# Summing the modulation vectors of a two-layer encoder over partitions: a GpSimd all-reduce in place of TensorE transposes and matmuls with ones

## The chip, the cores and the metric

The kernel runs on one core of a Trainium2 chip. The metric is the device time of one execution in microseconds (us), the median of the runs shown. The engines are named as the profile names them: PE is TensorE, PEld its weight loads, DVE is VectorE, ACT is ScalarE, POOL is GpSimd, and SP is SyncE, whose queue issues all DMAs here.

## What is computed

A bidirectional encoder of two layers on 256 tokens of 1024 channels, in float32. Each layer first makes six modulation vectors of 1024 channels from one conditioning vector `c`, and uses them around a mixer (three kinds of attention) and a SwiGLU feed-forward part:

```python
mod = jax.nn.silu(c) @ ada_w + ada_b                     # (1024,) @ (1024, 6*1024)
sh_m, sc_m, g_m, sh_f, sc_f, g_f = split(mod, 6)         # m = 0 .. 5 in the kernel
h = rms_norm(x, norm_mix_g) * (1 + sc_m) + sh_m
proj = h @ w_in                                          # three attentions and three gates follow
x = x + g_m * (merged @ w_out)
h = rms_norm(x, norm_ffn_g) * (1 + sc_f) + sh_f
gate, up = split(h @ ffn_w_gate_up)
x = x + g_f * ((silu(gate) * up) @ ffn_w_down)
```

## The kernel before, in words

**The stream of weights.** All projections are one list of *items*, each two 128-row chunks of a weight matrix by 512 columns. An item is loaded by SP into one of five `raw` buffers (512 KB), split by ACT into a rounded part `whi` and by DVE into the rest `wlo` (`split_to`, L215 and L216), and read by PE in three matmuls a chunk (L305 to L307) for each of the two token tiles. There are seven buffers of `whi` and of `wlo`, so DVE may split some items ahead of PE. PE works on the second token tile four items behind the first (`LAG = 4`). Two items' worth of steps, one for each token tile, move the counter `cur`; `later(k, fn)` defers a piece of code by `k` such steps. Beside the items stand pieces of attention, put at items by `at`. A scheduler then orders each engine's instructions; every engine works through its own list in order.

**The modulation vectors.** One matrix of 1024 by 1024 belongs to each vector m. It is taken in two halves of 512 columns, and each half in four units (`ada_units`): a unit loads 256 rows into a `raw` buffer of the same five, and DVE multiplies each row chunk by its value of silu(c) and adds it to `acc`, 128 partitions by 512 columns (L137, L139). What is left after the fourth unit is to add the 128 partitions of `acc` (`fin`). Two ways are used:
- m = 0, 1, 3, 4 are needed with the channel on the partition. `col_mod` transposes the four 128-column blocks of `acc` on PE (L121), and DVE adds along the free axis out of PSUM (L123) and adds the bias. This happens `DG = 4` steps later.
- m = 2 and 5 are needed as rows, the same on every partition. `acc` is split into two parts (ACT L215, DVE L216), and PE multiplies both with a matrix of ones (L201, L202), which sums and copies to all partitions at once; DVE adds the bias row out of PSUM (L203).

**Where the units stand.** In each layer the six halves of m = 2, 4, 3 are spread over the items of the gates and attention. Layer 0 then takes the two halves of its m = 5 and the four of layer 1's m = 1 and 0 during its feed-forward part; layer 1 takes the two of its own m = 5 there. That makes 20 halves: 8 as rows, 12 as columns. The first vectors of layer 0 are made by other functions in quarters, at the kernel's start, and are not touched here except for one buffer.

I call the stretches **A** (layer 0's attention, about 90 to 205 us, six halves), **B** (layer 0's feed-forward, about 265 to 375 us, six halves), **C** (layer 1's attention, about 495 to 610 us, a repeat of A with six halves) and **D** (layer 1's feed-forward, about 690 to 780 us, two halves).

**POOL** has little to do: it makes the small reciprocal roots of the norms by a power (L107), the rotary tables, the attention bias, and, right behind A and C, the sums of the three branches (`post_br`, L708), whose result PE transposes (L717).

Of the kernel before, what the change touches and what calls it, by code (L numbers as in the profile page):

```python
# [15 lines left out]
P = 128  # L16
# [16 lines left out]
DO = 2  # L33
DG = 4
DN = 4
# [3 lines left out]
def encoder_kernel(ctx: ExitStack, tc: tile.TileContext, x, consts, cols, rows, ada_b, rpb, ada_w, w_in,  # L39
                   w_uq, w_ukv, w_na, w_mla, w_gqa, w_out, w_gu, w_dn, fng, out):  # L40
    nc = tc.nc

# [1 line left out]
    cpool = ctx.enter_context(tc.tile_pool(name="cpool", bufs=1))  # L44
# [4 lines left out]
    s2p = ctx.enter_context(tc.tile_pool(name="s2p", bufs=2))  # L49
    tmp = ctx.enter_context(tc.tile_pool(name="tmp", bufs=6))  # L50
    ppl = ctx.enter_context(tc.tile_pool(name="ppl", bufs=4))
# [8 lines left out]
    def nm(s):  # L60
        uid[0] += 1
        return f"{s}_{uid[0]}"
# [12 lines left out]

# [1 line left out]
    x_sb = cpool.tile([P, NT, D], F32, name="x_sb")  # L77
# [23 lines left out]
    def colp(l, kind, j0, n):  # L101
        base = KC + l * 64 + {"b": 0, "gm": 48, "gf": 56}[kind]
        return cols_sb[:, base + j0: base + j0 + n]
# [5 lines left out]

# [1 line left out]
    mods = {}  # L111

    def col_mod(l, m, j0, n, acc):
        """Sums acc [128, n*128] over its partitions into columns j0..j0+n of the modulation (channel on partition)."""
        if (l, m) not in mods:
            mods[(l, m)] = modp.tile([P, KC], F32, tag=f"c{m}", name=nm("cm"))
        dst = mods[(l, m)][:, j0:j0 + n]
        ps = tpb()
        pv = ps.rearrange("p (j q) -> p j q", j=4)
        for j in range(n):  # L120
            nc.tensor.transpose(pv[:, j, :], acc[:, j * P:(j + 1) * P], ident)  # L121
        red = sm(4)[:, 0:n]
        nc.vector.tensor_reduce(out=red, in_=pv[:, 0:n, :], op=ALU.add, axis=AX.X)  # L123
        bcol = colp(l, "b", m * KC + j0, n)
        if m in (1, 4):
            r2 = sm(4)[:, 0:n]
            nc.vector.tensor_tensor(out=r2, in0=red, in1=bcol, op=ALU.add)
            g = colp(l, "gm" if m == 1 else "gf", j0, n)
            nc.vector.scalar_tensor_tensor(out=dst, in0=r2, scalar=1.0, in1=g, op0=ALU.add, op1=ALU.mult)
        else:  # L130
            nc.vector.tensor_tensor(out=dst, in0=red, in1=bcol, op=ALU.add)

    def ada_acc(acc, raw, kc0, nk):
# [22 lines left out]
    def ada_quarter_pe(l, m, q, raws):  # L156
# [3 lines left out]
        for kc in range(KC):  # L160
            nc.tensor.matmul(ps[0:1, 0:256], sc[:, kc:kc + 1], raws[(m, kc // 4)][:, kc % 4, :], start=(kc == 0),
                             stop=(kc == KC - 1))
        row = smp.tile([1, 256], F32, tag="row", name=nm("row"), bufs=1)
        nc.scalar.copy(row, ps[0:1, 0:256])
# [6 lines left out]
    def ada_units(l, m, hf, row):  # L171
# [14 lines left out]
        def fin():  # L186
            acc = st["acc"]
            if not row:
                later(DG, lambda: col_mod(l, m, hf * 4, 4, acc))
                return  # L190
            if hf == 0:
                mods[(l, m)] = modp.tile([P, D], F32, tag="G", name=nm("G"), bufs=1)
            bb = t2([P, 512])
            c0 = m * D + hf * 512
            nc.sync.dma_start(bb, ada_b[l, c0:c0 + 512].partition_broadcast(P))
            ah, al = t2([P, 512], F32R), t2([P, 512], F32R)
            split_to(ah, al, acc)

            def b_():
                ps = tpb()  # L200
                nc.tensor.matmul(ps, onesr, ah, start=True, stop=False)  # L201
                nc.tensor.matmul(ps, onesr, al, start=False, stop=True)  # L202
                nc.vector.tensor_tensor(out=mods[(l, m)][:, hf * 512:(hf + 1) * 512], in0=ps, in1=bb, op=ALU.add)  # L203

            later(DG, b_)

        return [unit(u) for u in range(4)]

# [1 line left out]
    def act_tiles():  # L210
# [49 lines left out]

# [1 line left out]
    items = []  # L262
# [22 lines left out]
    def group(units_src, nkc, n, lhs, post, kc0=0, pres=None):  # L285
        """units_src(u): DRAM sources of unit u (two contraction chunks); lhs(t, part, kc): stationary operand."""
        ps = {}
# [37 lines left out]
    def later(k, fn):  # L325
        deferred.append((cur[0] + k, fn))
# [10 lines left out]

    # ================= layers =================
    ssn = {}
# [6 lines left out]
    def layer(l):  # L346
# [4 lines left out]

# [1 line left out]
        def params():  # L353
# [40 lines left out]

# [1 line left out]
        def post_g1(t, ps):  # L396
# [50 lines left out]
        def rope64(dst, tmpv, xin, C, Sg, H):  # L447
            """dst = x*C + swap16(x)*S over H heads of 64"""
            xv = xin.rearrange("p (h d) -> p h d", h=H)
# [125 lines left out]

# [1 line left out]
        def attn_head(branch, h):  # L577
# [115 lines left out]

# [1 line left out]
        st["m"] = {}  # L695
# [37 lines left out]

# [1 line left out]
        def post_res(key, m, after, half=None):  # L735
# [28 lines left out]

# [1 line left out]
        st["hid"] = {}  # L766
# [70 lines left out]

# [1 line left out]
        def spread(units, a, b):  # L839
# [16 lines left out]

# [1 line left out]
    state[0] = {"hT": None}  # L858
# [143 lines left out]
```

## Time and profile before

| what | value |
|---|---|
| time, median of 3 runs | 851.92 us (850.71 to 852.44) |
| span of the profiled execution | 852.1 us |
| PE busy | 809.9 us, 95% |
| DVE busy | 612.1 us, 72% |
| ACT busy | 426.4 us, 50% |
| POOL busy | 85.0 us, 10% |
| DMA, mean rate | 220 GB/s |

The profiled execution has no time of its own besides its span. An engine's busy time is the sum of its instructions' own durations where they don't overlap; an idle engine costs only where something waits for it.

### The profile page before, as it was taken

Reading aid. Unit: us, or ns where it says so; the run is one execution under the profiler, and the core shown is the slowest. Engines: PE = TensorE matmul, PEld = TensorE weight load, DVE = VectorE, ACT = ScalarE, POOL = GpSimd, SP = SyncE. Lnnn points to the kernel's source line nnn. Section 1 sums busy time; section 2 is a strip of 40 time slices with the busy share of each in tenths; the row PEclk is TensorE's granted clock in tenths of the full one; section 3 lists DMA queues with packets and bytes.
Section 4 is the critical chain, followed back from the end, with each engine's and each line's share of the span. In section 5 each row is a group of like instructions: output and inputs, shape, how many; then the busy total and the mean of one; then the engine's idle time right before and its main releaser. Section 6 shows DMA issues by size and latency. Waiting matters only on the chain.

```text
span 852.1 us, 10916 instructions
## 1 busy us (share of the span) xinstructions
PE 809.9 (95%) x3842; PEld 654.0 (77%) x3842; DVE 612.1 (72%) x910; ACT 426.4 (50%) x725; POOL 85.0 (10%) x110
## 2 busy tenths in 40 slices
PE   3779999999999999999999999999999999999996
PEld 2348787888778887788878888788877788888884
DVE  4848998688867878785566698868886666665562
ACT  3346654444366443444457665544437644444341
POOL 1142120002400000000032001000240000000010
PEclk9999999999999999999999999999999999999998
DMA  9968677678555998985774667767755567775531
GB/s 317 348 154 271 188 237 245 221 224 266 178 173 166 317 305 281 308 270 188 207 216 141 178 187 240 248 217 222 259 186 173 178 222 255 249 232 178 191 102 50
DMA packets 112871, 187.21 MB, mean 220 GB/s; under 512 B 14384, under 2 KB 33456, under 8 KB 112816
## 3 DMA queue, kind: packets, MB, share of 16 engines
q1 hardware_dynamic: 112816, 186.51, 69.3%
q8 instruction: 30, 0.49, 0.2%
q14 instruction: 25, 0.20, 0.1%
HBM read 185.44 MB, written 1.05 MB: 219 GB/s over the span
## 4 chain that ended last, share of the span: by engine, by line
PE 76%; DVE 9%; DMA 7%; issue 4%; ACT 3%; POOL 2%; POOLq 0%; DVEq 0%; SPq 0%; ACTq 0%
PE mm L305 21%; PE mm L307 20%; PE mm L306 20%; DMA raw<-in_ada_w_dram 6%; PE tp L598 4%; DVE wlo L216 3%; PE o L654 3%; DVE acc L139 3%; PE tp L633 2%; PE mm L298 1%; ACT tm L246 1%; PE tp L237 1%; PE tp L779 1%; PE tp L121 1%; ACT hi L215 1%
## 5 line engine op out<-in xcount | busy, mean ns | idle before, releaser
L215 ACT CAST whi<-raw 128x1024 fp32r<-128x1024 f32 (+2 forms) x240 | 249.8, 1044 | 266.4 <-PE mm L307 191.4
L216 DVE TENSOR_TENSOR wlo<-raw,whi 128x1024 fp32r<-128x1024 f32 (+2 forms) x240 | 300.0, 1256 | 102.0 <-ACT whi L215 101.6
L305 PE MATMUL mm<-whi,hi 128*128 128x512 f32 (+1 forms) x768 | 306.5, 399 | 0.6 <-ACT hi L215 0.6
L306 PE MATMUL mm<-wlo,hi 128*128 128x512 f32 (+1 forms) x768 | 299.8, 390 | 2.2 <-DVE wlo L216 2.1
L307 PE MATMUL mm<-whi,lo 128*128 128x512 f32 (+1 forms) x768 | 300.1, 391 | 0.7 <-DVE lo L721 0.5
L307 PEld LDWEIGHTS mm<-whi,lo 128*128 128x128 f32 x768 | 144.2, 188 | 32.9 <-DVE lo L216 1.7
L306 PEld LDWEIGHTS mm<-wlo,hi 128*128 128x128 f32 x768 | 144.5, 188 | 30.6 <-DVE wlo L216 3.7
L305 PEld LDWEIGHTS mm<-whi,hi 128*128 128x128 f32 x768 | 144.3, 188 | 30.6 <-issue 2.6
L139 DVE SCALAR_TENSOR_TENSOR acc<-raw,sc,acc 128x512 f32<-128x512 f32 x140 | 104.6, 747 | 37.2 <-DMA raw<-in_ada_w_dram 35.4
L305 PE MATMUL mm<-whi,s 128*128 128x512 f32 (+1 forms) x188 | 73.6, 391 | 0.0
L306 PE MATMUL mm<-wlo,s 128*128 128x512 f32 (+1 forms) x188 | 72.8, 387 | 0.0
L307 PE MATMUL mm<-whi,s 128*128 128x512 f32 (+1 forms) x188 | 72.8, 388 | 0.0
L708 POOL TENSOR_TENSOR tm<-tm,tm 128x512 f32<-128x512 f32 x16 | 28.7, 1793 | 211.1 <-DVE tm L707 205.0
L307 PEld LDWEIGHTS mm<-whi,s 128*128 128x128 f32 x188 | 35.3, 188 | 7.1
L306 PEld LDWEIGHTS mm<-wlo,s 128*128 128x128 f32 x188 | 35.3, 188 | 6.9
L305 PEld LDWEIGHTS mm<-whi,s 128*128 128x128 f32 x188 | 35.3, 188 | 6.8
L384 POOL TENSOR_TENSOR s<-s,con 128x256 f32<-128x256 f32 x16 | 15.6, 1003 | 176.2 <-DMA s<-in_rpb_dram 168.6
L624 ACT ACTIVATE P<-tp,sm,rq 128x256 f32<-128x256 f32 x32 | 17.7, 558 | 27.1 <-DVE sm L619 23.7
L298 PE MATMUL mm<-raw,hF 128*128 128x416 f32 (+1 forms) x64 | 28.6, 599 | 0.0
L237 PE MATMUL tp<-con,tm 128*128 128x128 f32 x64 | 10.1, 313 | 16.7 <-DVE tm L230 16.7
L654 PEld LDWEIGHTS o<-s,PT 128*128 128x128 f32 x192 | 24.2, 191 | 1.1
L107 POOL TENSOR_TENSOR sm<-sm,nhalf 128x1 f32<-128x1 f32 (+2 forms) x22 | 18.3, 833 | 64.4 <-DVE sm L469 33.1
(145 smaller groups left out, 719.4 us busy)
## 6 DMA issues: line engine op xcount, KB each, us to landing
raw<-in_ada_w_dram SPq DMA_DIRECT2D x80, 512.0 KB, 4.8
raw<-in_w_gu_dram SPq DMA_DIRECT2D x80, 512.0 KB, 4.4
raw<-in_w_in_dram SPq DMA_DIRECT2D x64, 512.0 KB, 4.3
raw<-in_w_dn_dram SPq DMA_DIRECT2D x44, 512.0 KB, 4.8
s<-in_ada_w_dram SPq DMA_DIRECT2D x16, 512.0 KB, 9.4
raw<-in_w_out_dram SPq DMA_DIRECT2D x16, 512.0 KB, 4.5
raw<-in_w_in_dram SPq DMA_DIRECT2D x16, 256.0 KB, 3.2
raw<-in_w_gqa_dram SPq DMA_DIRECT2D x8, 512.0 KB, 5.4
```

The lines of the kernel that those rows point to most:

```text
L107: nc.gpsimd.tensor_tensor(out=r, in0=ms, in1=nhalf[:, 0:n], op=ALU.pow)
L139: nc.vector.scalar_tensor_tensor(out=acc, in0=raw[:, j, :], scalar=sc[:, kc:kc + 1], in1=acc, op0=ALU.mult, op1=ALU.add)
L215: nc.scalar.copy(hi_ap, src)
L216: nc.vector.tensor_tensor(out=lo_ap, in0=src, in1=hi_ap.bitcast(F32), op=ALU.subtract)
L237: nc.tensor.transpose(pv[:, j, :], xs[:, j * P:(j + 1) * P], ident)
L298: nc.tensor.matmul(ps[t][:, 0:n], state["hF"][kc // 4][:, kc % 4, t * P:(t + 1) * P], it["w"][:, j, 0:n], start=(kc == 0), stop=(kc == nkc ...
L305: nc.tensor.matmul(ps[t][:, 0:n], lhs(t, 0, kc), hi[:, j, 0:n], start=first, stop=False)
L306: nc.tensor.matmul(ps[t][:, 0:n], lhs(t, 0, kc), lo[:, j, 0:n], start=False, stop=False)
L307: nc.tensor.matmul(ps[t][:, 0:n], lhs(t, 1, kc), hi[:, j, 0:n], start=False, stop=last)
L598: nc.tensor.matmul(sv[:, t, :], q(t), k, start=True, stop=True)
L654: nc.tensor.matmul(ov[:, t, hs, :], ptT[:, k, t * P:(t + 1) * P], v, start=(k == 0), stop=(k == NT - 1))
L708: nc.gpsimd.tensor_tensor(out=m, in0=m, in1=y, op=ALU.add)
```

## The change

For all 20 halves the sum over partitions becomes one GpSimd instruction, `partition_all_reduce`, from `acc` into a new tile `tot` (128 by 512, the sum on every partition). For the rows the bias is added to `tot` directly. For the columns `diag_mod` multiplies `tot` by the identity matrix in each 128-column block and adds along the free axis, so that partition p keeps channel p. The readers of `tot` are put 10 steps behind instead of 4. The pool of work tiles `tmp` (tag `tm`) gets a seventh buffer, and the small `row` tile of the start moves into it. Other lines of the diff are comments.

```diff
-DG = 4
+DG = 10
...
-    tmp = ctx.enter_context(tc.tile_pool(name="tmp", bufs=6))
+    tmp = ctx.enter_context(tc.tile_pool(name="tmp", bufs=7))
...
+    def diag_mod(l, m, j0, tot):
...
+        dst = mods[(l, m)][:, j0:j0 + 4]
+        tv = tot.rearrange("p (j q) -> p j q", j=4)
+        nc.vector.tensor_tensor(out=tv, in0=tv, in1=ident.unsqueeze(1).to_broadcast([P, 4, P]), op=ALU.mult)
+        red = sm(4)
+        nc.vector.tensor_reduce(out=red, in_=tv, op=ALU.add, axis=AX.X)
+        add_bias(l, m, j0, 4, red, dst)
...
-        row = smp.tile([1, 256], F32, tag="row", name=nm("row"), bufs=1)
+        row = t2([1, 256])
...
         def fin():
             acc = st["acc"]
+            tot = t2([P, 512])
+            nc.gpsimd.partition_all_reduce(tot, acc, P, bass.bass_isa.ReduceOp.add)
             if not row:
-                later(DG, lambda: col_mod(l, m, hf * 4, 4, acc))
+                later(DG, lambda: diag_mod(l, m, hf * 4, tot))
                 return
...
-            ah, al = t2([P, 512], F32R), t2([P, 512], F32R)
-            split_to(ah, al, acc)
-
-            def b_():
-                ps = tpb()
-                nc.tensor.matmul(ps, onesr, ah, start=True, stop=False)
-                nc.tensor.matmul(ps, onesr, al, start=False, stop=True)
-                nc.vector.tensor_tensor(out=mods[(l, m)][:, hf * 512:(hf + 1) * 512], in0=ps, in1=bb, op=ALU.add)
-
-            later(DG, b_)
+            later(DG, lambda: nc.vector.tensor_tensor(out=mods[(l, m)][:, hf * 512:(hf + 1) * 512], in0=tot, in1=bb,
+                                                      op=ALU.add))
```

In the program that is built, POOL's list shows the change at the end of stretch A like this. Before, its last table instruction (L367) is followed by the branch sums (L708):

```order
L361 TENSOR_TENSOR gC_3918<-con,rw_3916 128x128
L107 TENSOR_TENSOR sm_923<-sm_921,nhalf 128x8
L499 TENSOR_SCALAR rq_273<-sm_923 128x8
L367 TENSOR_TENSOR gS_3919<-con,rw_3916 128x2x16 x4
L708 TENSOR_TENSOR tm_1808<-tm_1808,tm_1842 128x512
L708 TENSOR_TENSOR tm_1808<-tm_1808,tm_1891 128x512
```

Now, at the same place (line numbers are eight higher, L375 is the table, L716 the branch sums, L203 the all-reduces):

```order
L375 TENSOR_TENSOR gS_3883<-con,rw_3880 128x2x16 x4
L203 ISA
L203 ISA tm_1141<-acc_1043 128x512
L203 ISA tm_1308<-acc_1181 128x512
L203 ISA tm_1479<-acc_1354 128x512
L203 ISA tm_1609<-acc_1519 128x512
L203 ISA tm_1742<-acc_1643 128x512
L203 ISA tm_1851<-acc_1765 128x512
L716 ISA
L716 TENSOR_TENSOR tm_1796<-tm_1796,tm_1821 128x512
L716 TENSOR_TENSOR tm_1796<-tm_1796,tm_1872 128x512
```

Six sums have moved in ahead of the branch sums, and the two `ISA` rows without a tile are instructions that change the library of POOL's code, one before the first sum and one behind the last. The whole program has eight more of those than before.

On DVE in stretch B, before, the list around the end of one half reads (`acc_2922` ends with the second row; the rows behind it belong to the next half and to the weight items):

```order
L216 TENSOR_TENSOR wlo_3017<-raw_3014,whi_3016 128x1024
L139 SCALAR_TENSOR_TENSOR acc_2922<-raw_3032,sc,acc_2922 128x512
L137 TENSOR_SCALAR acc_3058<-raw_3059,sc 128x512
L139 SCALAR_TENSOR_TENSOR acc_3058<-raw_3059,sc,acc_3058 128x512
L216 TENSOR_TENSOR wlo_3039<-raw_3036,whi_3038 128x1024
L216 TENSOR_TENSOR s_720_2982<-tp_2977,s_720_2982 128x512
L216 TENSOR_TENSOR wlo_3066<-raw_3063,whi_3065 128x1024
L139 SCALAR_TENSOR_TENSOR acc_3058<-raw_3119,sc,acc_3058 128x512 x2
```

Now the same place reads (the half's `acc` is `acc_2896`, its sum `tm_3006`; the weight split is L224, the accumulation L151 and L153):

```order
L153 SCALAR_TENSOR_TENSOR acc_2896<-raw_3002,sc,acc_2896 128x512
L151 TENSOR_SCALAR acc_3030<-raw_3031,sc 128x512
L153 SCALAR_TENSOR_TENSOR acc_3030<-raw_3031,sc,acc_3030 128x512
L224 TENSOR_TENSOR wlo_3011<-raw_3008,whi_3010 128x1024
L224 TENSOR_TENSOR s_709_2945<-tp_2940,s_709_2945 128x512
L142 TENSOR_TENSOR tm_3006<-tm_3006,con 128x512
L144 TENSOR_REDUCE sm_3142<-tm_3006 128x4
L224 TENSOR_TENSOR wlo_3038<-raw_3035,whi_3037 128x1024
```

The first reader of the sum (L142) stands four instructions behind the last write of `acc`, and a weight split is right behind it. PE's list is the same as before but for the 16 matmuls with ones and the 48 transposes, which are gone; SP's list is the same.

## Rows read from the trace of the kernel before

**Rows 1.** The page: span, and busy time by engine.
```profile
span 852.1 us, 10916 instructions
...
PE 809.9 (95%) x3842; PEld 654.0 (77%) x3842; DVE 612.1 (72%) x910; ACT 426.4 (50%) x725; POOL 85.0 (10%) x110
```

**Rows 2.** Windows: busy time by engine (instructions) in stretches A, B, D.
```profile
core 0: us, PE busy (x) PEld busy (x) DVE busy (x) ACT busy (x) POOL busy (x), PEclk, DMA share, GB/s
90.00:205.00 115.00, 115.00 (x615) 94.81 (x615) 96.22 (x149) 60.66 (x124) 6.17 (x9) 1.00 0.74 232
265.00:375.00 110.00, 108.75 (x498) 88.96 (x497) 89.10 (x113) 48.13 (x57) 0.00 (x0) 1.00 0.86 288
690.00:780.00 90.00, 90.00 (x413) 74.40 (x413) 59.25 (x65) 42.71 (x50) 0.00 (x0) 1.00 0.71 230
```

**Rows 3.** Chain of waits within stretch A, share by line.
```profile
by line: PE mm L305 21.5%; PE mm L306 21.1%; PE mm L307 20.9%; PE tp L598 12.5%; PE o L654 11.7%; PE tp L633 7.0%; PE tp L670 1.5%; PE tp L121 1.2%; PE tp L516 0.9%; PE tp L507 0.8%; PE tp L201 0.5%; PE tp L202 0.4%; PE tp L482 0.2%
```

**Rows 4.** Chain of waits within stretch B, share by line.
```profile
by line: DMA raw<-in_ada_w_dram 40.3%; DVE wlo L216 17.8%; issue 11.0%; DVE acc L139 7.9%; DMA raw<-in_w_gu_dram 5.5%; PE mm L306 4.0%; PE mm L307 3.5%; PE mm L305 3.5%; DVE tm L772 2.7%; DVE s L216 1.1%; DVE G L203 0.9%; DVE tm L216 0.5%; 
```

**Rows 5.** Chain of waits within stretch D, share by line.
```profile
by line: PE mm L307 31.9%; PE mm L305 31.7%; PE mm L306 31.6%; PE tp L779 3.9%; PE tp L201 0.5%; PE tp L202 0.5%
```

**Rows 6.** Windows of the `wlo` tiles alone: PE reads, weight loads, DVE writes.
```profile
60.00:150.00 90.00, 32.81 (x84) 15.90 (x85) 32.03 (x26) 1.00 0.74 229
60.00:190.00 130.00, 46.56 (x120) 22.61 (x120) 43.02 (x35) 1.00 0.72 227
60.00:345.00 285.00, 127.29 (x326) 61.34 (x326) 106.88 (x85) 1.00 0.73 235
```

**Rows 7.** Timeline of PE around one column half: start, duration, instruction.
```profile
375.01 0.39 PE L307 MATMUL mm<-whi,lo 128*128 128x512 f32 x1
375.24 0.60 PE L121 MATMUL tp<-con,acc 128*128 128x128 f32 x4
...
376.14 0.40 PE L307 MATMUL mm<-whi,lo 128*128 128x512 f32 x1
```

**Rows 8.** Timeline of PE around one row half.
```profile
767.79 0.40 PE L307 MATMUL mm<-whi,lo 128*128 128x512 f32 x1
768.02 0.40 PE L201 MATMUL tp<-tm,onesr 128*128 128x512 f32 x1
...
768.97 0.40 PE L307 MATMUL mm<-whi,lo 128*128 128x512 f32 x1
```

**Rows 9.** Instructions of tile `acc`: count, duration in ns (min/median/max).
```profile
L216 DVE TENSOR_TENSOR tm<-acc,tm x8: 680/690/693, 116.0 to 754.8; 128x512 fp32r<-128x512 f32 x8
```

**Rows 10.** Timeline of POOL: a power and two branch sums.
```profile
88.02 1.74 POOL L107 TENSOR_TENSOR sm<-sm,nhalf 128x8 f32<-128x8 f32 x1 [2.68 <-DVE sm L497]
...
202.55 1.29 POOL L708 TENSOR_TENSOR tm<-tm,tm 128x512 f32<-128x512 f32 x1 [91.38 <-DVE tm L707]
206.87 2.15 POOL L708 TENSOR_TENSOR tm<-tm,tm 128x512 f32<-128x512 f32 x1 [3.04 <-DVE tm L707]
```

**Rows 11.** Timeline of DVE at the end of stretch A.
```profile
194.52 1.54 DVE L139 SCALAR_TENSOR_TENSOR acc<-raw,sc,acc 128x512 f32<-128x512 f32 x2 [0.71 <-DMA raw<-in_ada_w_dram]
195.98 1.22 DVE L216 TENSOR_TENSOR wlo<-raw,whi 128x1024 fp32r<-128x1024 f32 x1
...
203.05 1.87 DVE L216 TENSOR_TENSOR wlo<-raw,whi 128x1024 fp32r<-128x1024 f32 x1 [0.65 <-ACT whi L215]
```

**Rows 12.** Timeline of PE: the first transposes of a branch sum.
```profile
210.39 0.60 PE L717 MATMUL tp<-con,tm 128*128 128x128 f32 x4
```

**Rows 13.** POOL's first instruction and its library load, by line L225 and timeline.
```profile
L225 POOLq MODIFY_POOL_CONFIG  x2: 11/11/11, 0.7 to 0.8; - x2
...
11.11 0.29 POOL L225 TENSOR_SCALAR sm<-ss 128x1 f32<-128x1 f32 x1 [10.68 <-ACT tm L220]
```

**Rows 14.** Timeline of DVE in stretch B, at the end of one half.
```profile
334.30 0.75 DVE L139 SCALAR_TENSOR_TENSOR acc<-raw,sc,acc 128x512 f32<-128x512 f32 x1
...
337.28 0.68 DVE L216 TENSOR_TENSOR s<-tp,s 128x512 fp32r<-128x512 f32 x1
```

More of the change, by code (lines that the diff above doesn't have):

```diff
@@ L123, in col_mod, with add_bias @@
         nc.vector.tensor_reduce(out=red, in_=pv[:, 0:n, :], op=ALU.add, axis=AX.X)
+        add_bias(l, m, j0, n, red, dst)
+    def add_bias(l, m, j0, n, red, dst):
         bcol = colp(l, "b", m * KC + j0, n)
@@ L131, in col_mod @@
             nc.vector.tensor_tensor(out=dst, in0=red, in1=bcol, op=ALU.add)
+    def diag_mod(l, m, j0, tot):
+        if (l, m) not in mods:
+            mods[(l, m)] = modp.tile([P, KC], F32, tag=f"c{m}", name=nm("cm"))
+        dst = mods[(l, m)][:, j0:j0 + 4]
[4 more added lines that the diff above has]
+        add_bias(l, m, j0, 4, red, dst)
     def ada_acc(acc, raw, kc0, nk):
```

## The prediction

> **What bounds the kernel now.** The page comes first [rows 1]: PE is busy for 809.9 of 852.1 us. Its granted clock is at the upper of its levels, 2.4 GHz, in A, B and D [rows 2], so no term below rests on the clock. But 95% is a mean, and the stretches differ. The windows and the chain of waits, asked for each stretch, show it. In A the chain is PE from end to end [rows 3], and PE is busy for all 115.0 us while DVE is free for 115.0 - 96.2 = 18.8 us [rows 2]. C repeats A, and I give it the same numbers. In D the chain is again PE alone [rows 5], with DVE free for 90.0 - 59.3 = 30.7 us. In B it is different [rows 4]: PE holds 11%, loads into `raw` 46%, and DVE's weight splits and accumulations 26%. PE is hardly idle there (108.8 of 110.0 us), but it gets its tiles at the last moment. DVE's free 110.0 - 89.1 = 20.9 us are waits for loads, which in their turn wait for DVE to free a buffer.
>
> How far DVE is ahead can be counted from the `wlo` tiles [rows 6]: each is read by four matmuls, and because PE takes the second token tile four items later, DVE is three tiles ahead of a quarter of the reads even if PE takes every tile the moment it is written. At 150 us it is 26 - 84/4 = 5, so two tiles to spare; at 345 us 85 - 326/4 = 3.5, half a tile. In A a tile lasts PE (190 - 150)/(35 - 26) = 4.4 us, so two tiles are 8.8 us of cover.
>
> **What the change removes.** Two matmuls with ones: from 767.79 to 768.97 us PE starts three ordinary matmuls and the pair [rows 8]; a matmul goes by in 0.23 us (375.01 to 375.24 us) [rows 7], so the pair costs 1.18 - 0.69 = 0.49 us. Four transposes: from 375.01 to 376.14 us there are three matmuls and the set, 1.13 - 0.69 = 0.44 us. A and C each lose two pairs and four sets, 2.7 us; B the same; D two pairs, 1.0 us. Where the chain is PE this comes off in full; in B next to nothing does, and I count nothing. At most 2.7 + 2.7 + 1.0 = 6.4 us are to be gained, down to 845.7. ACT loses eight casts, worth nothing since it is idle for half of the time [rows 1], and DVE eight subtractions of 0.69 us [rows 9].
>
> **What it adds on DVE.** Each of the 12 column halves gets a multiplication of 128x512 with two inputs in SBUF; the nearest row is the subtraction, 0.69 us. The reduction behind it and the bias stay. A, B and C each get four of these and lose two subtractions: +1.4 us of DVE.
>
> **What a sum costs.** No row shows an all-reduce. From below it is at least one pass over 128x512 on POOL, 1.29 us; from above the slowest thing that POOL does per column is the power, 1.74 us for 8 columns, 0.22 us each, which for 512 columns is 111 us [rows 10]. An all-reduce only adds, so the branch sum (an add of the same shape) is the nearer row. It must bring partial sums together and hand the result back, two passes; where POOL and DVE meet a pass takes 2.15 us, so I take 2 x 2.15 = 4.3 us as an estimate. If instead 128 values are halved seven times with a pass each, it is 7 x 1.29 = 9.0 us.
>
> **What it does to DVE.** One row matters most. A branch sum on POOL runs from 202.55 to 203.84 us [rows 10]; the weight split on DVE that starts at 203.05 takes 1.87 us instead of 1.22 and ends 1.08 us after POOL's end [rows 11]. It waited until POOL was done. So a split, or any DVE instruction with two inputs in SBUF (the accumulations too), stands still while POOL reads. The Trainium skill states this rule in SBUF — State Buffer, section Who interferes with whom: the second DVE read port is GpSimd's only one, and the loser is blocked for the whole instruction. The trace agrees, with the 0.65 us above, but only for a plain add; no row tells whether an all-reduce holds the port throughout.
>
> I take it that it does: then DVE, in order, loses about the sum's duration each time, 6 x 4.3 + 1.4 = 27.2 us in A, B and C each, 2 x 4.3 - 1.4 = 7.2 us in D.
> - A and C: 27.2 - 18.8 = 8.4 us are not covered by free time, and the 8.8 us of tiles in hand cover them. Price nothing; without the tiles, 8.4 us each.
> - D: 7.2 of 30.7 us free. Nothing.
> - B: if all 20.9 us of free time can be used, 27.2 - 20.9 = 6.3 us are left; if none, 27.2 us. Loads still land during a stall but no buffer is freed and no further load issued, so I take the middle, 16.8 us.
>
> **What it adds on POOL.** The sums and library loads stand in POOL's list ahead of the branch sums behind A and C. The last `acc` of A is done at 196.06 us [rows 11], and PE transposes the first branch sum at 210.39 [rows 12], for which POOL must have done two, 1.29 + 2.15 = 3.4 us. That leaves 210.39 - 196.06 - 3.4 = 10.9 us for the last sum and the library load. The load has no row of its own: its two instructions stand at 0.7 us and 11 ns each, and POOL's first work begins at 11.11 us, released by ACT [rows 13]. So it costs between 0 and 10.3 us. Half, 5.2 us, with 4.3 makes 9.5, under 10.9: no price. At the upper end it is 3.7 us late in A and in C.
>
> The wait for the sum itself: in B the shortest way from the last write of an `acc` (335.05 us) to where its reader now stands (337.96) is 2.9 us [rows 14]. DVE waits there for what is left of 4.3 us, but this is the same stall, not a second one. No load moves in SP's list, and the seventh `tm` buffer stands for the one that `tot` keeps longer: no price for either.
>
> **Sum.** 852.1 - 2.7 (A) + 16.8 (B) - 2.7 (C) - 1.0 (D) = 862.5 us. The profiled span is 0.2 us above the median of the runs, so the same holds for the median.
>
> **Rivals.**
> 1. *POOL holds the port only briefly, or the sum is shorter* (the other side). If it reads its columns in one pass and exchanges between its cores without the port, a stall is 1.3 us or less: 6 x 1.3 + 1.4 = 9.2 us in B, within the 20.9 us free. Then PE's saving stands, 845.7 us, or 850.3 if half of the stalls count. It decides at the point where half of B's stalls equals the 6.4 us: stalls of (12.8 - 1.4)/6 = 1.9 us. For it: PE's chain in A, C and D, and nothing on POOL in B [rows 2]. Against it: the split at 203.05 us.
> 2. *The sum is long.* At 9.0 us: A and C 55.4 - 18.8 - 8.8 - 2.7 = 25.1 us each, B between 34.5 and 55.4, so 45.0, D -1.0: 946 us. At 6 us the same sum gives 892. For it: 128 partitions are seven halvings. Against it: plain adds on POOL are quick. The Trainium skill, GPSIMD Engine Reference, section Cross-partition — where GPSIMD wins, gives 247.7 us for a `tensor_reduce` along partitions at 128x2048; a quarter of it, 62 us, would by this sum make an estimate of nearly 2000 us. No run here shows it, and it is another instruction; it has no more than a small part of this rival's chance.
> 3. *No change*: stalls near 1.9 us, or the late library loads eating A's and C's savings.
>
> **How the numbers follow.** Less than 0.2% (1.7 us) can't be told from no change here. Rival 1 has 0.40 (845 to 850), rival 3 0.08, the forecast (port held, a sum of 2.8 to 6 us: 855 to 892) 0.36, rival 2 0.16. Slower is thus the likelier sign, 0.52. The forecast's own range is 855 to 892. The range asked for reaches down to all of rival 1, a little below its floor, 843, and up into a sum of nearly 7 us, 905, and leaves out some 0.17.
>
> **What would show it.** Right: in B, DVE splits that start behind an all-reduce and last several us, PE idle on `wlo` there, and a B longer by 15 us or more, while A, C and D shrink by 1 to 3 us each. Wrong: splits at 1.22 us beside a running all-reduce (rival 1); DVE waiting for `tot` in A and C as well, and PE behind it (rival 2); PE waiting at the first L717 for POOL, with a gap in POOL's timeline behind the last sum (the library load). A sum's duration is the number on which most hangs: one us more costs about 6 us in B alone.

## The result, and the profile after

The changed kernel takes 857.18 us (median of 12 runs, 855.16 to 864.19), the kernel before beside it on the same chip 852.67 us (12 runs, 850.42 to 857.35). The ratio is 1.0063, with an interval of 1.0043 to 1.0082: slower by 0.6%, or 4.5 us. The forecast was 862.5 us, in a range of 843 to 905, with 0.52 for slower.

The profiled execution took 855.16 us, the quickest of the twelve; its span is only 1.2 us longer than that of the kernel before (853.4 against 852.1 [rows 1]), so its trace shows less than the whole loss. The first rows are the page's span and busy times; then the windows of A, B, C and D.

```profile
span 853.4 us, 10813 instructions
...
PE 804.7 (94%) x3778; PEld 647.4 (76%) x3778; DVE 640.3 (75%) x914; ACT 422.3 (49%) x717; POOL 157.3 (18%) x130
```
```profile
core 0: us, PE busy (x) PEld busy (x) DVE busy (x) ACT busy (x) POOL busy (x), PEclk, DMA share, GB/s
90.00:205.00 115.00, 113.12 (x593) 92.86 (x592) 104.65 (x150) 58.74 (x121) 25.55 (x13) 0.99 0.77 232
265.00:375.00 110.00, 106.03 (x478) 86.16 (x477) 98.50 (x114) 47.35 (x55) 21.82 (x6) 1.00 0.84 281
495.00:610.00 115.00, 113.88 (x602) 93.48 (x602) 105.15 (x156) 61.42 (x122) 25.85 (x10) 1.00 0.76 231
690.00:780.00 90.00, 90.00 (x414) 74.49 (x413) 60.12 (x63) 41.22 (x48) 8.06 (x2) 1.00 0.72 233
```

PE is busy for 5.2 us less than before [rows 1], and yet the end comes later. In A it was never idle [rows 2]; now it is idle for 1.9 us there, and DVE is busy for 8.4 us more. D is as it was. The chain of waits within A (first line) and within B (second line), share by line:

```profile
by line: PE mm L313 13.6%; PE mm L315 12.9%; PE mm L314 12.9%; PE tp L606 8.3%; issue 8.2%; PE o L662 7.3%; DVE wlo L224 7.3%; DMA tm<-in_ada_b_dram 5.3%; DMA raw<-in_ada_w_dram 4.8%; PE tp L641 4.5%; DVE acc L153 4.0%; DVE sm L617 2.2%; AC
by line: DMA raw<-in_ada_w_dram 22.0%; DVE wlo L224 20.3%; DMA raw<-in_w_gu_dram 10.0%; issue 8.9%; DVE acc L153 6.8%; PE mm L314 5.8%; PE mm L315 5.2%; PE mm L313 5.2%; DMA tm<-in_ada_b_dram 4.9%; ACT whi L223 3.6%; DVE acc L151 3.1%; DVE 
```

B's chain is of the same kind as before [rows 4]. A's is not [rows 3]: it was PE alone, and now holds DVE and loads as well. (Most lines have moved by 8: L305 is L313, L216 is L224, L598 is L606, L139 is L153, L717 is L725.) The waits of PE between 90 us and the end, longest sums first (us in total, times, longest), show where it now stands; the first fence is the changed kernel, the second the kernel before:

```profile
PE tp L725 <- POOL tm L716: 4.5, 3, 1.7
PE tp L245 <- DVE tm L238: 4.3, 6, 1.3
PE mm L314 <- DVE wlo L224: 4.0, 3, 2.0
PE tp L606 <- DVE lo L224: 2.5, 2, 1.6
```
```profile
PE tp L237 <- DVE tm L230: 4.1, 6, 1.2
PE tp L717 <- POOL tm L708: 3.3, 2, 1.7
PE mm L306 <- DVE wlo L216: 1.2, 2, 1.0
```

New are 2.8 us on `wlo`, 2.5 us on `lo` (the low part of a transposed attention output) and 1.2 us on the branch sums. The sums themselves are this group of the page's instructions (busy us, mean ns):

```profile
L203 POOL PARTITION_ALL_REDUCE tm<-acc x20 | 71.5, 3574 | 316.5 <-DVE acc L153 229.9 <-DVE sm L627 29.8 <-DVE cm L132 29.7
```

They take 3.57 us on average, 3.23 us for the shortest. The longer ones, up to 4.14 us, began while an instruction of DVE on `acc` or a weight split was still running, and ended 3.1 to 3.2 us after it. How one of them reaches PE shows in the timeline of A around the third sum (start, duration, instruction):

```profile
141.92 0.60 PE L678 MATMUL tp<-con,tm 128*128 128x128 f32 x4
142.08 3.23 POOL L203 PARTITION_ALL_REDUCE tm<-acc  x1 [14.15 <-DVE acc L153]
142.41 2.18 DVE L151 TENSOR_SCALAR acc<-raw,sc 128x512 f32<-128x512 f32 x1 [0.51 <-DMA raw<-in_ada_w_dram]
144.52 1.21 DVE L224 TENSOR_TENSOR wlo<-raw,whi 128x1024 fp32r<-128x1024 f32 x1
...
145.11 1.00 PE L662 MATMUL o<-s,PT 128*128 128x64 f32 x8
...
146.99 0.68 DVE L224 TENSOR_TENSOR lo<-tp,hi 128x512 fp32r<-128x512 f32 x1
...
147.72 0.55 ACT L632 ACTIVATE P<-tp,sm,rq 128x256 f32<-128x256 f32 x1
147.72 1.18 PE L606 MATMUL tp<-kcT,s 64*128 64x256 f32 x4 [1.61 <-DVE lo L224]
...
148.26 0.58 ACT L646 COPY PT<-tp 128x512 f32<-128x512 f32 x1
...
148.83 0.79 PE L313 MATMUL mm<-whi,hi 128*128 128x512 f32 x1
149.42 0.63 PE L314 MATMUL mm<-wlo,hi 128*128 128x512 f32 x1
```

L151 takes 0.48 us at its median; here it takes 2.18, because it stands behind the sum, and ends at 144.59 us, shortly ahead of the sum at 145.31. Everything behind it in DVE's order moves by 1.7 us: the split, and then the `lo` for which PE waits 1.61 us. L606 (the scores of attention) does not read `lo`. It writes into a `tp` buffer in PSUM, the memory that takes TensorE's results, and there are three of these: two are still to be read, by L632 and L646, and the third, which the transposes of L678 filled, comes free when `lo` has been made from it. Then the second price: the matmuls from 148.8 us on take 0.63 us and not 0.39. The windows around it (granted clock is the third number from the right):

```profile
145.00:148.70 3.70, 2.09 (x14) 1.60 (x12) 3.70 (x7) 1.54 (x5) 0.31 (x1) 1.00 0.49 138
148.70:152.10 3.40, 3.40 (x9) 2.60 (x9) 3.35 (x7) 1.39 (x3) 0.00 (x0) 0.50 0.82 216
152.10:155.00 2.90, 2.90 (x21) 2.54 (x20) 2.83 (x5) 1.84 (x5) 0.00 (x0) 1.00 0.79 249
```

TensorE went from 2.4 to 1.2 GHz (granted clock 0.50) after it had stood still, and 3.4 us at half speed are 1.7 us lost. The same happened from 230.6 to 234.0 us. Between 62 and 840 us the kernel before had no such stretch in its trace.

The following table is worked out from the traces: the same matmul on `wlo` (the k-th of each trace), its start less that in the trace of the kernel before, in us. The other columns are experiments told below (no sum with 4 steps, only B, sums unused, unused without the last, ones column). It is read by differences down a column, since the first line is only how the entry of each execution fell out. Each column is one execution, which need not lie at the median of its kernel.

```
start before  after  no sum,4st  only B      unused   unused,not last  ones col
    90.5       -1.2     +0.8        +0.1        -1.6           -1.0         +0.3
   163.0       +1.4     -0.1        +0.1        +3.8           +2.3         +0.3
   205.4       +0.2     -1.4        +0.1        +3.8           +2.3         +1.8
   265.1       +1.7     -2.4        +0.2        +5.7           +2.3         +2.2
   375.9       +2.1     -6.5        -2.0        +5.6           +3.2         +1.9
   495.5       +2.1     -6.4        -1.8        +6.3           +3.4         +2.0
   560.4       +2.6     -7.3        -1.8        +9.8           +9.4         +2.0
   610.4       +1.3     -8.6        -1.8        +9.8           +9.4         +3.5
   640.3       +2.1     -9.7        -1.8       +15.7           +9.4         +3.9
   780.1       +1.2    -10.7        -1.7       +15.7           +9.4         +3.9
```

### The profile page after: what moved, and what is told of

Same layout as the page of the kernel before. It is cut to its first block, busy times and chain, and to the rows that moved or that the text cites. A ratio compares the mean times of both kernels' runs of the same rounds, so it can differ in the third digit from the quotient of the medians.

```text
span 853.4 us, 10813 instructions
## 1 busy us (share of the span) xinstructions
PE 804.7 (94%) x3778; PEld 647.4 (76%) x3778; DVE 640.3 (75%) x914; ACT 422.3 (49%) x717; POOL 157.3 (18%) x130
## 4 chain that ended last, share of the span: by engine, by line
PE 65%; DVE 13%; DMA 8%; issue 6%; ACT 4%; POOL 2%; SPq 0%; POOLq 0%; DVEq 0%; ACTq 0%
PE mm L313 18%; PE mm L314 18%; PE mm L315 18%; DVE wlo L224 5%; DMA raw<-in_ada_w_dram 5%; DVE acc L153 3%; PE tp L606 3%; PE o L662 2%; ACT tm L254 1%; POOL tm L716 1%; DMA tm<-in_ada_b_dram 1%; DMA raw<-in_w_gu_dram 1%; PE tp L641 1%; ACT whi L223 1%; PE tp L245 1%
## 5 line engine op out<-in xcount | busy, mean ns | idle before, releaser
L224 DVE TENSOR_TENSOR wlo<-raw,whi 128x1024 fp32r<-128x1024 f32 (+2 forms) x240 | 309.6, 1298 | 88.1 <-ACT whi L223 87.9
L313 PE MATMUL mm<-whi,hi 128*128 128x512 f32 (+1 forms) x768 | 307.5, 401 | 0.6 <-ACT hi L223 0.6
L313 PEld LDWEIGHTS mm<-whi,hi 128*128 128x128 f32 x768 | 145.1, 189 | 30.7 <-issue 2.7
L203 POOL PARTITION_ALL_REDUCE tm<-acc x20 | 71.5, 3574 | 316.5 <-DVE acc L153 229.9
L153 DVE SCALAR_TENSOR_TENSOR acc<-raw,sc,acc 128x512 f32<-128x512 f32 x140 | 104.4, 746 | 30.7 <-DMA raw<-in_ada_w_dram 29.4
L313 PE MATMUL mm<-whi,s 128*128 128x512 f32 (+1 forms) x188 | 73.6, 391 | 0.0
L313 PEld LDWEIGHTS mm<-whi,s 128*128 128x128 f32 x188 | 35.3, 188 | 6.9
L716 POOL TENSOR_TENSOR tm<-tm,tm 128x512 f32<-128x512 f32 x16 | 29.6, 1852 | 34.7 <-DVE tm L715 25.8
L632 ACT ACTIVATE P<-tp,sm,rq 128x256 f32<-128x256 f32 x32 | 17.7, 559 | 25.5 <-DVE sm L627 19.8
```

The lines of the kernel that those rows point to most:

```text
L153: nc.vector.scalar_tensor_tensor(out=acc, in0=raw[:, j, :], scalar=sc[:, kc:kc + 1], in1=acc, op0=ALU.mult, op1=ALU.add)
L203: nc.gpsimd.partition_all_reduce(tot, acc, P, bass.bass_isa.ReduceOp.add)
L224: nc.vector.tensor_tensor(out=lo_ap, in0=src, in1=hi_ap.bitcast(F32), op=ALU.subtract)
L313: nc.tensor.matmul(ps[t][:, 0:n], lhs(t, 0, kc), hi[:, j, 0:n], start=first, stop=False)
L716: nc.gpsimd.tensor_tensor(out=m, in0=m, in1=y, op=ALU.add)
```

## The experiments

**Four first cuts** ran together; the kernel before stood at 853.95 us beside them (23 runs).

*No sum.* The readers take the unsummed accumulator; no GpSimd sum, no library.
```
-            tot = t2([P, 512])
-            nc.gpsimd.partition_all_reduce(tot, acc, P, bass.bass_isa.ReduceOp.add)
...
-                later(DG, lambda: diag_mod(l, m, hf * 4, tot))
+                later(DG, lambda: diag_mod(l, m, hf * 4, acc))
```


> This kernel leaves out the sum over partitions: diagonal and bias work on the unsummed accumulator, so POOL has no all-reduce and no library load, while TensorE's transposes and matmuls stay removed and DVE's extra multiplications stay in. Theory (the change's loss is DVE standing behind POOL's port): TensorE's saving is left alone, 846 us or 6 us below the kernel before. Rival (the saving was never there, or the multiplications on DVE cost it): 850 to 853 us, no better than before.

Measured 855.88 us, ratio 1.0022 (1.0001 to 1.0042). Neither theory said that. The trace names a fault of the experiment: with DG = 10 an accumulator, of which there are two, is now held for ten steps. DVE begins the next half at 184.20 us, when the old accumulator has been read at 183.00, and until then the weights of that half keep their `raw` buffer. The next modulation load waits for it in SP's queue, with all loads behind it (waits of SP, 178 to 187 us, and its timeline; L130, which the view names, ends within 0.1 us of the accumulation that frees the buffer):
```profile
SPq L195 <- DVE sm L130: 7.4, 1, 7.4
```
```profile
178.21 0.37 SPq L282 DMA_DIRECT2D raw<-in_w_in_dram  x1
185.96 0.37 SPq L195 DMA_DIRECT2D raw<-in_ada_w_dram  x1
```
In the changed kernel the sum itself frees the accumulator, so it doesn't have this wait. The run says nothing of the sums; its repair is below.

*A small sum.* Of each accumulator 8 of 512 columns are summed on GpSimd, the others are left unsummed; readers as in the run above.
```
-            nc.gpsimd.partition_all_reduce(tot, acc, P, bass.bass_isa.ReduceOp.add)
+            few = sm(8)
+            nc.gpsimd.partition_all_reduce(few, acc[:, 0:8], P, bass.bass_isa.ReduceOp.add)
```


> Each all-reduce is done on 8 of the 512 columns and its result added where the sum would be; the other 504 columns stay unsummed. Library loads, the order on POOL and the wait for POOL stay. Theory (port held during the sum): the port is held for a fraction of a us, so 847 to 850 us, close to the kernel without sums. Rival (late library loads and waits for POOL are the loss): as slow as the changed kernel, 855 to 858 us.

Measured 869.37 us, ratio 1.0182 (1.0155 to 1.0210): slower than with whole sums, against both. The accumulators are held for ten steps here too. In POOL's order the last sum of A and of C now stands behind the first branch sum. At the end of C, with PE's waits from 615 to 655 us:
```profile
605.33 0.82 POOL L205 PARTITION_ALL_REDUCE sm<-acc  x1 [37.62 <-DVE sm L146]
616.36 1.45 POOL L723 TENSOR_TENSOR tm<-tm,tm 128x512 f32<-128x512 f32 x1 [10.20 <-DVE wlo L231]
625.09 1.24 POOL L205 PARTITION_ALL_REDUCE sm<-acc  x1 [7.28 <-DVE wlo L231]
637.75 2.49 POOL L723 TENSOR_TENSOR tm<-tm,tm 128x512 f32<-128x512 f32 x2 [11.43 <-issue]
```
```profile
PE tp L732 <- POOL tm L723: 11.3, 2, 10.0
```
Each change between a sum and an ordinary instruction leaves a gap of 7 to 11 us, whichever way it goes, and PE waits 11.3 us for the branch sums, 10.0 of them at once. So a library change can stop PE when work stands close behind it; the changed kernel has one at the end of A and one at the end of C.

*Each sum twice.*
```
             nc.gpsimd.partition_all_reduce(tot, acc, P, bass.bass_isa.ReduceOp.add)
+            nc.gpsimd.partition_all_reduce(tot, acc, P, bass.bass_isa.ReduceOp.add)
```


> Each all-reduce is issued twice in a row, with the same result. Theory (port): DVE stands twice as long, 6 x 3.2 us more in each of A, B and C, which free time no longer covers: 870 to 890 us. Rival (library loads): the loads stay as many, one sum more is 3.2 us later at the end of A and C: 860 to 864 us.

Measured 889.06 us, ratio 1.0410 (1.0388 to 1.0432), as the theory had it: 31 us more than the changed kernel stands above the kernel before, for about 70 us more of sums. The time of a sum does count, and the second 70 us count for more than the first. That the first had the free time of DVE to fall into is argued, not shown; and some 10 of the 31 us are PE's waits for the branch sums, 14.3 us in place of 4.5, since the last sums end later.

*All but B.* The six sums of B go back to TensorE, with their own delay of 4 steps.
```
+            pool = (l, m) not in ((0, 5), (1, 1), (1, 0))
+            dg = DG if pool else 4
...
-                later(DG, lambda: diag_mod(l, m, hf * 4, tot))
+                later(dg, lambda: diag_mod(l, m, hf * 4, tot) if pool else col_mod(l, m, hf * 4, 4, acc))
```


> In stretch B the sums go back to TensorE (as before the change, 4 steps behind); A, C and D keep POOL. By the prediction B was the only stretch that loses: 846 us. Rival (A and C lose about what they save, as the shift of matmuls in the two profiles suggests, and B costs little): 853 to 856 us, little better than the changed kernel.

Measured 855.87 us, ratio 1.0024 (1.0005 to 1.0043). With B as before, the kernel is still slower, as the rival had it. The prediction's savings in A and C do not come out; what the sums cost stands there. (Worked out as in the table: +0.8 us in A and +3.2 in C, each with its branch sums, and -0.9 in D.) PE waits for `lo` in L621 (the changed kernel's L606) at the same two places, 1.6 us in A and 1.6 us in C, each followed by 1.2 GHz.

**Parts apart** ran together next; the kernel before at 853.66 us (23 runs).

*Only B.* As above with the condition turned round.
```
+            pool = (l, m) in ((0, 5), (1, 1), (1, 0))
```


> Sums on GpSimd in stretch B alone; A, C and D stay on TensorE with their own 4 steps of delay. The kernel before stood at 852 to 854 us. Prediction's step (B loses 16.8 us to stalls): 868 to 871. Rival (as in the trace after, B's stalls of about 4 us are nearly paid by TensorE work and weight-splitting time that B gets back): 852.5 to 855.

Measured 852.66 us, ratio 0.9998 (0.9981 to 1.0015), as the rival had it. The prediction's 16.8 us are not there. In the table B even gains 2.2 us in this trace; in the median it is no change. DVE is fuller in B than in either kernel, and PE is not idle for more than 1.1 us (window of B):
```profile
265.00:375.00 110.00, 108.88 (x489) 88.22 (x488) 101.61 (x118) 48.91 (x57) 21.91 (x6) 1.00 0.87 290
```

*No sum, 4 steps.* The first run repaired: `DG = 4`. Leaves out the sums.


> No sum over partitions at all, as in the first run without sums, but with 4 steps of delay, so that the accumulators (two buffers) are held no longer than before. Leaves out the sum over partitions. Theory (TensorE's saving is real in every stretch; in the run with 10 steps the held accumulators delayed the modulation loads at the ends of A and C and took it back): 844 to 848. Rival (A and C are set by transfers and VectorE, so TensorE's saving there is worth nothing): 849 to 852.

Measured 842.91 us, ratio 0.9876 (0.9852 to 0.9900): 10.7 us to be had, more than the theory said. By the table 3.2 us come from A with its branch sums, 4.1 from B, 3.3 from C with its branch sums and 1.0 from D. TensorE's work in B is worth its length too: its matmuls go in steps of 0.45 to 0.47 us, 2.7 us together, and a wait for `wlo` at 362.6 us, 1.0 us in the kernel before, is gone besides. A and C give some 0.5 us more than the 2.7 us counted for their matmuls; PE's idle stretches of 1.65 us among the branch sums (at 228.8 and 633.8 us of the kernel before) are down to 0.7. Against the first run, one number (10 steps to 4) is worth 13 us. In the two traces, whose spans are 7.5 us apart, PE waits from 90 us on for 8.0 us for `wlo` and `whi` with 10 steps and for 0.5 with 4, so the late loads behind the held accumulator are the likely cause. The bias rows are held longer too, and no run parts the two.

*Sums unused.* The kernel before, TensorE's sums and all, and the 20 GpSimd sums beside them into a tile that nobody reads. The small `row` tile of the start moves into the work tiles, as in the changed kernel.
```
+            idle = smp.tile([P, 512], F32, tag="idle", name=nm("idle"), bufs=1)
+            nc.gpsimd.partition_all_reduce(idle, acc, P, bass.bass_isa.ReduceOp.add)
             if not row:
                 later(DG, lambda: col_mod(l, m, hf * 4, 4, acc))
```


> The kernel before, with its TensorE sums, and the 20 GpSimd sums beside them, whose results nobody reads. Theory (the sums cost by the port, that is by the VectorE instructions that stand behind them, and by library changes, whoever reads the result): 860 to 866, the time before plus the 5 us lost plus the 6 us of TensorE that the change saved. Rival (the cost is in the change of order and in waits for the summed tile): 852 to 855.

Measured 869.39 us, ratio 1.0193 (1.0149 to 1.0238), above the theory's range. DVE works in the same order as in the kernel before, so no change of its order explains it. The sums cost 15.7 us though nobody reads them, and the books close: -10.7 + 15.7 = +5.0 us, against 4.5 measured for the change; since the interval of this run alone reaches from 12.7 to 20.3 us, that they close so well is in part luck. The cost lies where the table steps up: 5.4 us between 90 and 163 us and 3.5 between 495 and 560, 1.9 us at the end of A and 5.9 at the end of C. In the first two PE waits for `P` just ahead of the third sum (1.8 us in A, 1.0 in C), for `lo` behind it (1.9 us each, as in the timeline above), and in A 3.4 us at 1.2 GHz follow. At the ends of A and C the last sum is late, and the library change behind it makes the first branch sum late:
```profile
200.21 4.06 POOL L189 PARTITION_ALL_REDUCE idle<-acc  x1 [10.47 <-DVE acc L139]
212.51 5.80 POOL L710 TENSOR_TENSOR tm<-tm,tm 128x512 f32<-128x512 f32 x3 [8.24 <-DVE tm L705]
...
613.03 4.06 POOL L189 PARTITION_ALL_REDUCE idle<-acc  x1 [12.35 <-DVE acc L139]
625.97 4.76 POOL L710 TENSOR_TENSOR tm<-tm,tm 128x512 f32<-128x512 f32 x3 [8.88 <-DVE tm L705]
```
```profile
PE tp L719 <- POOL tm L710: 9.3, 4, 4.3
PE tp L600 <- DVE lo L218: 3.9, 2, 1.9
PE tp L635 <- ACT P L626: 2.8, 2, 1.8
```

*Loads only.* The same with `acc[:, 0:8]` into an 8-column tile. The orders of POOL and of DVE are the same as in the run above.


> As the run with unused sums, but each sum takes 8 of 512 columns (about 0.9 us in place of 3.2 to 4.1): the library changes and the order on GpSimd stay, the port is hardly held. Theory (the port costs): 852 to 855, and well under the run with full sums. Rival (library changes cost, the branch sums behind them come late): within 2 us of the run with full sums, 858 to 866.

Measured 856.32 us, ratio 1.0035 (1.0016 to 1.0054): 2.7 us. The sums' length is thus worth 13 of the 15.7 us, and library changes with twenty short sums 2.7. The time lies between the two ranges, 1.3 us above the theory's and 1.7 below the rival's; but the theory asked for a time well under the run with full sums and the rival for one within 2 us of it, and it is 13 us under it.

**A way out** came last; the kernel before at 854.63 us (21 runs).

*Ones column.* The kernel before without GpSimd sums; a column half is summed by four one-column matmuls and not by transposes and a reduction on DVE.
```
-            nc.tensor.transpose(pv[:, j, :], acc[:, j * P:(j + 1) * P], ident)
-        red = sm(4)[:, 0:n]
-        nc.vector.tensor_reduce(out=red, in_=pv[:, 0:n, :], op=ALU.add, axis=AX.X)
+            nc.tensor.matmul(ps[:, j:j + 1], acc[:, j * P:(j + 1) * P], ones[:, 0:1], start=True, stop=True)
```


> The kernel before without GpSimd sums; the four 128x128 transposes of a column modulation and VectorE's 128x512 reduction behind them are replaced by four matmuls of one column, the accumulator's 128 columns against a column of ones. The run without any sum gained 10.7 us. Theory (TensorE and VectorE time in these stretches is worth its full length, and the port is what spoils the change): 12 half modulations give back most of 0.44 us of TensorE each, and VectorE 0.68 us each: 847 to 850. Rival (the column matmuls load the same 128x128 weights and save little): 852 to 854.

Measured 859.69 us, ratio 1.0058 (1.0036 to 1.0080): slower, against both. The matmuls fall back by about 0.46 us at each half of A, B and C; only in B, where the waits for `wlo` at 362.6 us and earlier went (1.2 and 0.3 us in the matmuls' starts), is nothing of it left in the table. The instructions of the tile `ones` (ns min/median/max) say why:
```profile
L121 PEld LDWEIGHTS tp<-ones,acc x124: 186/192/337, 15.3 to 617.7; 128*128 128x128 f32 x124
L121 PE MATMUL tp<-ones,acc x124: 164/250/370, 15.6 to 617.7; 128*128 128x1 f32 x124
```
Before, the trace has 62 transposes in L121, with a weight load of 0.14 us each; now there are 124 matmuls of one column, each with a load of 0.19 us. The weights are loaded twice for each matmul. DVE's 0.68 us less for a half buy nothing in A and C, where PE's time counts; that they are what ended the waits in B is not shown.

*Unused, without the last.* The run with unused sums, less the last sum of A and of C.
```
+            if (m, hf) != (3, 1):
+                nc.gpsimd.partition_all_reduce(idle, acc, P, bass.bass_isa.ReduceOp.add)
```


> As the run with unused sums beside TensorE's (869.4, 15.7 us over the kernel before), without the last sum of A and of C, so that the standard library is loaded back before the branch sums. Theory (the port holds back VectorE in A and C, and the late branch sums cost what the trace shows behind them, 1.9 and 5.7 us): 860 to 864. Rival (the late branch sums cost nothing in the end): 867 to 870.

Measured 865.45 us, ratio 1.0130 (1.0101 to 1.0160), between the two ranges. The steps at the ends of A and C are gone: POOL has 16.4 us between the sum and the first branch sum, and PE's wait for the branch sums is the 3.3 us of the kernel before.
```profile
184.22 4.06 POOL L190 PARTITION_ALL_REDUCE idle<-acc  x1 [17.71 <-DVE acc L139]
204.68 1.29 POOL L711 TENSOR_TENSOR tm<-tm,tm 128x512 f32<-128x512 f32 x1 [16.40 <-DVE tm L710]
```
```profile
PE tp L601 <- DVE lo L219: 3.9, 2, 1.9
PE tp L720 <- POOL tm L711: 3.3, 2, 1.7
PE tp L636 <- ACT P L627: 1.8, 2, 1.3
```
The intervals of this run and of the one with all sums overlap, so the 3.9 us between their medians are not certain; the steps in the table are. What is left stands around the third sum of each: 3.3 and 6.0 us in the table, of which two waits for `lo` are 3.9 us, two for `P` 1.8, and 6.8 us at 1.2 GHz behind the second `lo` (558.5 to 565.3 us) 3.4.

*Hybrid.* GpSimd sums for the eight row halves only (`pool = row`), ones columns for the others.


> GpSimd sums only for the row modulations (8 of 20, the first two of each stretch, far from the branch sums); the column modulations by matmuls with a column of ones. Theory (a sum costs where VectorE is nearly full, and here 2 of them in A and 2 in C remain): 846 to 851, no better than the run with ones columns alone by more than 2 us. Rival (any GpSimd sum costs more than it saves): 852 to 856.

Measured 858.13 us, ratio 1.0051 (1.0033 to 1.0068), outside both ranges, since the ones columns cost what they cost in the run above. A has no step at 142 us here: its two sums come at 117.6 and 125.7 us, where nothing waits. In C PE waits 1.4 us for `lo` at the place of the third sum although none is near, so the place is tight in itself. Against the ones columns alone (859.69 us) the eight GpSimd sums make no difference that the intervals can tell.

*Last on PE.* The changed kernel, the last sum of A and of C by TensorE (`pool = (m, hf) != (3, 1)`).


> The changed kernel, with the last sum of A and of C on TensorE (4 steps), so that the standard library is back before the branch sums. Theory (late branch sums cost the changed kernel some of its loss): 852 to 855. Rival (the loss lies in the stalls at the port alone): 856 to 859.

Measured 858.06 us, ratio 1.0056 (1.0030 to 1.0081): the same as the changed kernel, as the rival had it. In the changed kernel the late library cost too little to be seen in the time, though this run also gives back what TensorE saved on two halves (0.9 us).

No version that computes the whole result beats the kernel before; only-B equals it.

## Why the prediction was right, and where it was not

The sign and the size came out, but the places didn't, and so the nearness of the number is luck: a cost in B that isn't there stood in for costs in A and C that were called covered and for the clock, and a saving was left out.

- **What TensorE saves.** 0.49 us for a pair and 0.44 for a set of four are borne out: the table falls by such steps in the run without sums. The wrong step is "in B next to nothing does, and I count nothing". B gave 4.1 us in that run's trace, and the whole kernel 10.7 in place of 6.4. That B's chain is made of loads and DVE [rows 4] does not make PE's time worthless there, since PE is busy for 108.8 of 110.0 us [rows 2].
- **What a sum takes.** 4.3 us was estimated, 3.57 is the mean. The size was near, but by an argument about two passes that no run bears out or refutes.
- **The port held throughout.** This was the step that was mis-sized. All 20 sums of the changed kernel have an instruction of DVE behind them, but DVE stands only from its own start to some 1.1 us before the sum's recorded end. Their lengths over the median of their lines add up to about 30 us, 1.5 us for a sum and not 4.3. That is below the 1.9 us at which rival 1 was to decide, and rival 1's time did not come either, for the next reason.
- **A and C covered.** This is the step that failed. The cover was counted in `wlo` tiles (8.8 us in hand) and in DVE's free time over the stretch (18.8 us). But what PE waited for at 147.7 us was a `tp` buffer, which a `lo` of attention had still to read, behind the held accumulation in DVE's order; of these there are three, and none was in hand. In every run that has the third sum of a whole accumulator in A and C, PE waits for `lo` behind it in A, in C or in both. One wait of 1.6 us there was followed by a stretch at 1.2 GHz, 1.7 us more. Against the run without sums, in these two traces, the sums cost the changed kernel 6.1 us in A with its branch sums (+2.9 in the table against -3.2), 3.3 in C, 4.5 in B and next to nothing in D.
- **B, 16.8 us.** The six stalls add up to 10.2 us by the count above, and DVE had 20.9 us free there. The price is 4.5 us against the run without sums, of which two idle stretches of PE at 300.6 and 339.7 us, behind `wlo`, are 2.0 and 1.7 us. Since B's own saving was 4.1, B is even, and the run with sums in B alone shows it.
- **D.** -1.0 us was predicted, and -0.9 us stands in the table.
- **Library load.** No price was given, with 10.9 us of room. The last sum of A ended at 198.42 us, and the first branch sum began at 206.79, 8.4 us later, some 4 us after its input was there. The price was small in the changed kernel, as the last run shows (PE's waits for the branch sums are 1.2 us longer); in the run with unused sums, where the sum came later, it was some 4 us by the medians (869.4 against 865.5). The Trainium skill, GPSIMD Engine Reference, section Instruction dispatch, gives about 6 us for the first call of a freshly loaded kernel. The gaps ahead of the first sums of A and C agree with it, 5.8 and 6.5 us, with the input there for 5.1 and 4.6 of them; those behind the last sums, 8.4 and 8.0 us, are longer.
- **The clock** was left out ("no term below rests on the clock"), and by an estimate it is most of the measured loss. In the profiled execution of the changed kernel two stretches at 1.2 GHz cost 3.4 us, and its runs spread from 855 to 864 us with the granted clock falling from 0.991 to 0.979. The estimate takes for every run the missing share of its granted clock times its span: 11.6 us on average over the changed kernel's 12 runs (mean clock 0.986), 7.9 us over the 23 runs of the kernel before that stood beside the first experiments (0.991). That is 3.7 of the 4.4 us between their means; without it the two kernels are nearly even, 846.8 and 846.2 us. The estimate counts all of TensorE's lost time as the kernel's, which no run shows by itself. By the same estimate the run without sums (835.8) and the one with unused sums (859.4) lie apart for other reasons than the clock.

Still open: when an idle PE loses its clock. The idle 1.66 us before L725 at 228.8 us was followed by 1.2 GHz in the changed kernel, and 1.65 us at the same place was not in the kernel before; nor was the 1.99 us at 300.6. No run moves the third sum of A and C alone, so its cost is read from the traces and not shown by an experiment.

## What to carry to other kernels

Work that is moved off a full engine is paid where it meets an in-order queue: ask not only how much free time DVE has over the stretch, but which instruction stands right behind the held one and whether the engine that waits for it has a tile or a PSUM buffer in hand. Separate gain and cost by two kernels, one without the work (here -10.7 us) and one where the new way runs beside the old, unread (here +15.7): here they add up to the change within the spread of the runs, and say which half to mend. Compare the granted clock of all runs and not of the profiled one alone: a short wait of TensorE can cost as much again in clock (here 1.61 us of waiting and 1.7 us behind it). Before a tile is held for longer, count its buffers: ten steps in place of four cost 13 us in the kernel without sums.

## What the hardware showed unexpectedly

- A sum over partitions of 128x512 f32 on GpSimd takes 3.23 to 4.14 us in the changed kernel, and one of 128x8 0.40 to 1.30 us in the run with short sums. The first blocks DVE until about 1.1 us before its recorded end.
- What it blocks is not only instructions with two inputs in SBUF: L151, which scales one, took 2.18 us for 0.48. The Trainium skill, SBUF — State Buffer, section Who interferes with whom, lists `tensor_scalar` among those that can take the shared ports; the trace agrees. A DVE instruction with an input in PSUM went by in its usual time: L617, which reads `tp`, takes 0.68 us beside the sum below, and the small L623 behind it, all in SBUF, takes 1.49 in place of 0.16.
```profile
123.53 1.22 DVE L224 TENSOR_TENSOR wlo<-raw,whi 128x1024 fp32r<-128x1024 f32 x1
123.79 4.14 POOL L203 PARTITION_ALL_REDUCE tm<-acc  x1 [4.34 <-DVE acc L153]
124.66 0.68 DVE L617 TENSOR_REDUCE sm<-tp 128x2 f32<-128x512 f32 x1
125.38 1.49 DVE L623 TENSOR_SCALAR sm<-sm 128x2 f32<-128x2 f32 x1
```
- An f32 matmul of one column costs more than a 128-column transpose, by 0.46 us for four: it loads its weights twice (124 loads of 0.19 us for 62 operations, where the transposes have 62 of 0.14).
- Going back from a sum to an ordinary GpSimd instruction is a library change as well, with a gap of 8.0 and 8.4 us in the changed kernel and 7.8 to 11.4 us where sums and branch sums alternate.
